# Layer 0's adaLN scale and shift as float32 products on four 32-column strips of TensorE, the first four units pipelined over slices of the scale

## The chip, the cores and the metric

The kernel runs on one core of a Trainium2 chip. The metric is the device time of one execution in microseconds (us). Tensors are float32. Large products are made from two rounded halves of each operand (`hh`, `hl` for the activations, `wh`, `wl` for the weights), as three matmuls `hh*wh + hl*wh + hh*wl` that accumulate in PSUM; "a product" of a unit below is one such matmul.

## The reference, cut to what matters

Two layers, each on 512 latent and 256 context tokens of width 2048:

```python
mod = jax.nn.silu(cond) @ w_ada + b_ada            # cond: c for the latents, c_ctx for the context
shift, scale, gate = jnp.split(mod, 3, axis=-1)    # 3 x 2048 values for each of the two
h = rms_norm(x, norm_w) * (1 + scale) + shift
p = h @ w_in                                       # 2048 x 6144: pool, gates, q, k, v
...                                                # pooling mixer and differential attention
x = x + gate * (merged @ w_out)
```

The change touches `scale` and `shift` of layer 0 alone: two vectors of 2048 values, each the product of a 2 x 2048 matrix (the two conditions) with a 2048 x 2048 block of `w_ada` (16.8 MB).

## The kernel before

The weights `w_in` are cut into 48 units of 128 columns for each layer; a unit is 16 steps over the contraction (k), each with three products for 512 latent and three for 256 context tokens, 96 matmuls in all. `ordered` (L66) chains everything on TensorE into the order in which the program issues it, and adds the cost of each to a planned clock. Side streams (generators) get a turn in `tick` when that clock has passed their due time. The kernel is scheduled at build time into one fixed order for each engine; each engine's queue, and SyncE's queue of DMA issues, runs strictly in that order.

**Start (`startup`, L885).** The order is a string of steps, `SS` (L1160). The scale comes in eight slices of 256 channels (`front(c)`, L929). `SK` makes them by turns in two ways. Slices 0, 2, 4, 6 ("P") load `w_sc0` and multiply on TensorE: per slice 16 float32 matmuls with two weight columns (the two conditions), tile `ads`, a row copy on ScalarE (`adr`) and two transposes (`adt`). Slices 1, 3, 5, 7 ("S") load the transposed `w_sct0` as eight 128 x 512 tiles; VectorE multiplies and sums each for one condition (`asq`, L953), GpSimd multiplies for the other (L957), and ScalarE sums that (L958). `fin(c)` (L980) closes a slice: bias, `acol`, then `hh`, `hl` of two k-steps from `xT` (L994 on ScalarE, L995 on VectorE). `proj` multiplies units 0 to 3 for these k-steps into `su` and `su_sc` (PSUM), since all four are accumulated at once. `N` computes the RMS roots from the squares (`ssq`), `S` spreads them over the tokens (`rsb`, `rstd`). `K` does the last three k-steps and evacuates (`vp`, L724).

**Shift (`shift_stream`, L272, over `mod_sums`, L212).** A side stream that begins at `H`, near the start's end. For each of 64 tiles of 128 x 512 (`swsh`) VectorE multiplies and sums for one condition (`jksh`, L258), GpSimd multiplies for the other (L260) and ScalarE sums (L261). The 64 sums close in groups of four channel blocks into two extra columns of `hh` and `hl` (columns 768 and 769). Units 4 to 7 (pooling values) need no shift. The first gate unit, unit 8 (`pj` with 258 columns), does.

**Pooling.** After each pooling unit, `pool_front` runs window sums on VectorE (two of eight on GpSimd); `pool_mix` multiplies them by `pool_w` (`mx`) and ScalarE evacuates (`M`). Weights of a unit are split by ScalarE (`wh_i`, L167) and VectorE (`wl_i`, L168). From unit 8 on, `gate_rows` and later `scale_shift` use `mod_sums` for the other adaLN parts.

Of the kernel before, what the change touches and what calls it, by code (L numbers as in the profile page):

```python
# [38 lines left out]
def tile_hybrid_block(ctx: ExitStack, tc, xc, xt, cc, w_in, w_out, w_sc0, w_sct0, w_sh0, w_mod0, w_mod1, b_col, norm_col,  # L39
# [99 lines left out]
    nc.vector.tensor_tensor(csil, csil, ctmp, ALU.mult)  # L139

# [71 lines left out]
    def mod_sums(nm, srcs, conds, tot, close, pace=None, extra=None):  # L212
        n = len(srcs)
        ahead = [0]
# [3 lines left out]
        def load(i):  # L218
            if i < 4 * n:
                ring = extra[1]() if extra else [(wpool, "wa", 2)]  # L220
                pool, tag, bufs = ring[i % len(ring)]
                ahead[0] = len(ring) - 1 if extra else 1
                w = pool.tile([P, 512], F32, tag=tag, name=f"sw{nm}_{i}", bufs=bufs)
                (queued if extra else behind)(nc.sync.dma_start(w, srcs[i % n][i // n]))
                tiles[i] = w

        load(0)
        while len(tiles) < ahead[0]:
            load(len(tiles))
        cs = slice(conds[0], conds[-1] + 1)  # L230
        rot = [(wpool, "ac0"), (wpool, "ac1")] + ([(extra[0], "p2")] if extra else [])
        cts = {}

        def load_c(c, s):
            if s < 4:
                pool, tag = rot[(2 * s + c) % 3 if extra else c]
                cts[c, s] = pool.tile([P, 512], F32, tag=tag, name=f"ct{c}_{nm}_{s}")
                (queued if extra else behind)(nc.sync.dma_start(cts[c, s].rearrange("p (k q) -> p k q", q=P),
                                                                csil_d[4 * s:4 * s + 4, c, :].partition_broadcast(P)))

        for s in range(4):
            for c in conds:
                if (c, s) not in cts:
                    load_c(c, s)
            ct = [cts.get((c, s)) for c in range(2)]
            if not (extra and s):
                yield -(SH[1] if extra else LA[3])
            dst = part if s else tot
            for j in range(n):
                i = s * n + j  # L250
                while len(tiles) <= ahead[0] and i + len(tiles) < 4 * n:
                    load(i + len(tiles))
                w = tiles.pop(s * n + j)
                for c in conds:
                    acc = dst[:, j, c:c + 1]
                    scratch = w if c == conds[-1] else (extra[2] if extra else wide_tile)(f"jk{nm}_{s}_{j}")
# [9 lines left out]
                if extra and j in (n // 2, n - 1):  # L266
                    load_c(0 if j < n - 1 else 1, s + 1)
                yield -(pace or LA[phase[0]])
# [5 lines left out]
    def shift_stream(ap, pace, ring, scratch):  # L274
        shcol = const.tile([P, KC, 2], F32, tag="ctmp", name="shcol")

        def close(j):
            v = shcol[:, j:j + 4]
            nc.vector.tensor_tensor(v, v, bcol[:, 0, j:j + 4, 0].unsqueeze(2).to_broadcast([P, 4, 2]), ALU.add)
            for k in range(j, j + 4):  # L280
                split(shcol[:, k, :], hh[k][:, TOK:], hl[k][:, TOK:])
            if j == 12:
                tables[0] = layer_tables(0)

        yield from mod_sums("sh", [w_sh0[j] for j in range(KC)], (0, 1), shcol, close, pace, (ap, ring, scratch))
# [71 lines left out]
    def phase_in(l):  # L357
# [499 lines left out]
    def startup(ap, pj, pscore, units, finish):  # L857
        kinds = SK
# [50 lines left out]
        ring = ["q0", "q1", "k0"]  # L909
        state = {}  # L910
        cnt = {"P": 0, "S": 0}

        def ws_tile(c, k, n):
            r = kinds[c]
            if c == 0 and k < 6:
                if k == 0:
                    state["w0"] = hpool.tile([P, 6, 256], F32, tag="hl0", name="ws0")
                w = state["w0"][:, k:k + n]
                queued(nc.sync.dma_start(w, w_sc0[c, :, k:k + n, :]))
                return w  # L920
            if c == 0 and k >= 12:
                tag = "G1" if k == 12 else "vh"
            else:
                tag = ring[cnt[r] % len(ring)]
                cnt[r] += 1
            w = ap.tile([P, n, 256], F32, tag=tag, name=f"ws{c}_{k}")
            queued(nc.sync.dma_start(w, w_sc0[c, :, k:k + n, :]))
            return w

        def front(c):  # L930
            kind = kinds[c]
            if kind == "P":
                ps = misc(f"ads{c}")
                for k0 in range(0, KC, 3):
                    n = min(3, KC - k0)
                    w = ws_tile(c, k0, n)
                    for j in range(n):
                        k = k0 + j
                        mm(ps[:2, :256], csil[:, k, :], w[:, j, :], k == 0, k == KC - 1)
                    yield  # L940
                row = wpool.tile([P, TOK], F32, tag="wx", name=f"adr{c}")[:2, :256]
                nc.scalar.activation(row, ps[:2, :256], AF.Copy)
                state[c] = row
                return
            acc = const.tile([P, 2, 2, 4], F32, tag="as", name=f"as{c}", bufs=2)
            for s in range(4):
                for j in range(2):
                    pool, tag = ((wpool, "wa"), (ap, "tmp"), (wpool, "ac0"), (wpool, "wa"), (ap, "tmp"), (wpool, "ac1"))[cnt["S"] % 6]
                    cnt["S"] += 1
                    w = pool.tile([P, 512], F32, tag=tag, name=f"ws{c}_{s}{j}", bufs=1 if tag[:2] == "ac" else 2)  # L950
                    queued(nc.sync.dma_start(w, w_sct0[2 * c + j, s]))
                    sq = wpool.tile([P, 512], F32, tag="wp", name=f"asq{c}_{s}{j}")
                    nc.vector.scalar_tensor_tensor(sq, w, 1.0, spread[0, s], ALU.mult, ALU.mult, accum_out=acc[:, j, 0, s:s + 1])  # L953
                    if (2 * s + j) % SD[0] == 1:
                        nc.vector.scalar_tensor_tensor(w, w, 1.0, spread[1, s], ALU.mult, ALU.mult, accum_out=acc[:, j, 1, s:s + 1])
                    else:
                        nc.gpsimd.tensor_tensor(w, w, spread[1, s], ALU.mult)  # L957
                        nc.scalar.activation(w, w, AF.Copy, accum_out=acc[:, j, 1, s:s + 1])  # L958
                    yield
            state[c] = acc  # L960

        spread = {}

        def spread_in():
            for i, (big_, last) in enumerate((("ah", "fq"), ("al", "fk"))):
                t = ap.tile([P, 3, 512], F32, tag=big_, name=f"csB{i}")
                u = ap.tile([P, 512], F32, tag=last, name=f"csC{i}")
                for d, k0, k1 in ((t, 0, 12), (u, 12, 16)):
                    d = d.rearrange("p s (k q) -> p (s k) q", q=P) if k0 == 0 else d.rearrange("p (k q) -> p k q", q=P)
                    queued(nc.sync.dma_start(d, csil_d[k0:k1, i, :].partition_broadcast(P)))  # L970
                for s in range(3):
                    spread[i, s] = t[:, s]
                spread[i, 3] = u

        def fin(c):
            with tc.high_priority(offset=1000):
                a = acol[0][:, 2 * c:2 * c + 2]
                if kinds[c] == "P":
                    pt = misc(f"adt{c}")
                    transposes(pt, [state[c][:, i * P:(i + 1) * P] for i in range(2)], 2)  # L980
                    total = pt[:, :4].rearrange("p (k c) -> p k c", c=2)
                else:
                    total = a
                    nc.vector.tensor_reduce(a, state[c], AX.X, ALU.add)
                nc.vector.tensor_tensor(a, total,
# [295 lines left out]
```

## Time and profile before

| | us |
|---|---|
| three timed runs | 2438.93, 2442.76, 2444.49 |
| their median | 2442.76 |
| the profiled execution, first to last instruction | 2437.6 |
| from start to unit 4's first product | 152.5 |
| from there to unit 8's first product | 117.4 |
| from there to 336 us | 66.1 |
| the rest | 2101.6 |

The page gives no time for the profiled execution other than its span, which is 5.2 us under the median. All times below that name a place are us from the span's start.

How to read it: TensorE (PE) is the engine that sets the end; behind 336 us the program issues the same work in both kernels. So the first three stretches of the table are read one by one: what the engine did there, and what it waited for. A busy share on another engine costs nothing by itself; it costs what PE waits for it.

### The profile page before, as it was taken

The numbers are of one execution on the slowest core, as the hardware profiler recorded it, in microseconds if no ns is written. First come the engines' busy times: TensorE is split into PE (matmuls) and PEld (weight loads), VectorE is DVE, ScalarE is ACT, GpSimd is POOL, SyncE is SP. The second block draws the span as 40 slices with busy tenths as digits, with TensorE's granted clock in tenths as the row PEclk, the third lists the DMA queues.
The fourth block names the chain that finished last, engine by engine and source line by source line (L and its number), as shares of the span: only waits on it lengthen the run. The fifth ranks groups of instructions, "written<-read, shape, count | busy, mean of one in ns | idle before, by whom it ended". The sixth has DMA issues, their size and how long they took to land.

```text
span 2437.6 us, 35303 instructions
## 1 busy us (share of the span) xinstructions
PE 2301.9 (94%) x12411; PEld 1916.9 (79%) x12411; DVE 1568.5 (64%) x2942; ACT 1206.3 (49%) x2586; POOL 637.0 (26%) x574
## 2 busy tenths in 40 slices
PE   6777799999999999998989999999999999999999
PEld 3566688888888888887767788788888888887787
DVE  5799955567767767777533468665666566666433
ACT  4544444455555555656555556223555445555321
POOL 2666645312122122122676720001120000000000
PEclk9888899999999999999999999999999999999999
DMA  8645455433333233234665555564333222224643
GB/s 277 205 154 157 133 172 165 122 104 109 92 102 108 87 111 104 81 90 137 203 192 186 182 174 147 178 193 143 102 115 92 69 66 63 63 68 129 198 135 116
DMA packets 194178, 324.27 MB, mean 133 GB/s; under 512 B 20993, under 2 KB 50257, under 8 KB 194001
## 3 DMA queue, kind: packets, MB, share of 16 engines
q1 hardware_dynamic: 194000, 322.03, 44.1%
q8 instruction: 97, 1.59, 0.3%
q14 instruction: 81, 0.66, 0.1%
HBM read 291.50 MB, written 24.16 MB: 129 GB/s over the span
## 4 chain that ended last, share of the span: by engine, by line
PE 50%; DMA 6%; DVE 4%; ACT 3%; POOL 3%; issue 2%; SPq 0%; DVEq 0%; POOLq 0%; ACTq 0%
PE pj L89 32%; PE ob L89 9%; PE sc L89 3%; DMA swss<-in_w_mod 3%; PE po L89 2%; POOL jkss L260 1%; PE at L98 1%; PE eb L89 1%; POOL swss L260 1%; DMA wr_o<-in_w_out 1%; DMA wr_m<-merged_d 1%; PE qt L98 1%; DMA xr<-in_xc 1%; ACT p L584 1%; DVE wl_i L168 1%
## 5 line engine op out<-in xcount | busy, mean ns | idle before, releaser
L89 PE MATMUL pj<-hh,wh_i 128*128 128x512 f32 (+2 forms) x2368 | 861.3, 364 | 23.4 <-DVE vp L724 16.1
L89 PE MATMUL pj<-hl,wh_i 128*128 128x512 f32 (+2 forms) x2368 | 831.4, 351 | 6.2 <-DVE hl L168 6.2
L89 PE MATMUL pj<-hh,wl_i 128*128 128x512 f32 (+2 forms) x2368 | 832.0, 351 | 1.1 <-DVE wl_i L168 1.1
L89 PEld LDWEIGHTS pj<-hh,wh_i 128*128 128x128 f32 x2368 | 450.7, 190 | 90.6 <-ACT wh_i L167 16.5
L89 PEld LDWEIGHTS pj<-hh,wl_i 128*128 128x128 f32 x2368 | 450.3, 190 | 64.3 <-DVE wl_i L168 1.5
L89 PEld LDWEIGHTS pj<-hl,wh_i 128*128 128x128 f32 x2368 | 451.1, 191 | 58.1 <-DVE hl L168 6.9
L168 DVE TENSOR_TENSOR wl_i<-wr_i,wh_i 128x512 fp32r<-128x512 f32 x352 | 269.9, 772 | 120.2 <-ACT wh_i L167 113.9
L167 ACT ACTIVATE wh_i<-wr_i 128x512 fp32r<-128x512 f32 x352 | 220.0, 628 | 248.9 <-PE pj L89 177.0
L89 PE MATMUL ob<-wh_o,hh 128*128 128x512 f32 x640 | 256.5, 401 | 17.9 <-DVE X L1119 14.3
L89 PE MATMUL ob<-wh_o,hl 128*128 128x512 f32 x640 | 254.5, 398 | 0.0
L89 PE MATMUL ob<-wl_o,hh 128*128 128x512 f32 x640 | 254.3, 397 | 0.0
L260 POOL TENSOR_TENSOR swss<-swss,ct_ss 128x512 f32<-128x512 f32 x128 | 181.5, 1418 | 265.8 <-DVE jkss L258 99.8
L168 DVE TENSOR_TENSOR wl_o<-wr_o,wh_o 128x512 fp32r<-128x512 f32 x144 | 105.1, 732 | 194.0 <-ACT wh_o L167 193.6
L260 POOL TENSOR_TENSOR swg<-swg,ct_g 128x512 f32<-128x512 f32 x88 | 123.3, 1403 | 313.9 <-DMA swg<-in_w_mod 105.6
L584 ACT ACTIVATE p<-sc,st,psc 128x768 f32<-128x768 f32 (+1 forms) x160 | 143.4, 901 | 57.5 <-DVE st L580 32.6
L89 PEld LDWEIGHTS ob<-wh_o,hh 128*128 128x128 f32 x640 | 121.5, 190 | 50.3 <-DVE X L1119 18.0
L579 DVE TENSOR_REDUCE st<-sc 128x2 f32<-128x1536 f32 (+1 forms) x80 | 123.3, 1541 | 58.7 <-PE sc L89 58.4
L167 ACT ACTIVATE wh_o<-wr_o 128x512 fp32r<-128x512 f32 x144 | 90.0, 626 | 131.3 <-PE ob L89 94.0
L89 PEld LDWEIGHTS ob<-wh_o,hl 128*128 128x128 f32 x640 | 121.4, 190 | 28.5
L89 PEld LDWEIGHTS ob<-wl_o,hh 128*128 128x128 f32 x640 | 121.8, 190 | 27.5
L589 POOL COPY r<-st 128x1 f32<-128x1 f32 x80 | 17.1, 214 | 478.8 <-DVE st L586 478.8
L260 POOL TENSOR_TENSOR swsh<-swsh,ct_sh 128x512 f32<-128x512 f32 x64 | 106.5, 1674 | 52.1 <-DVE jksh L258 19.1
(288 smaller groups left out, 3620.1 us busy)
## 6 DMA issues: line engine op xcount, KB each, us to landing
wr_i<-in_w_in SPq DMA_DIRECT2D x352, 256.0 KB, 2.7
wr_o<-in_w_out SPq DMA_DIRECT2D x144, 256.0 KB, 2.8
swg<-in_w_mod SPq DMA_DIRECT2D x128, 256.0 KB, 2.9
swss<-in_w_mod SPq DMA_DIRECT2D x128, 256.0 KB, 2.9
swsh<-in_w_sh SPq DMA_DIRECT2D x64, 256.0 KB, 2.8
ws<-in_w_sct SPq DMA_DIRECT2D x32, 256.0 KB, 5.0
wr_m<-merged_d SPq DMA_DIRECT2D x32, 256.0 KB, 2.7
wr_e<-in_w_in SPq DMA_DIRECT2D x32, 256.0 KB, 2.8
```

Of the source, the lines that this page charges most:

```text
L89: ordered(nc.tensor.matmul(out, a, b, start=start, stop=stop), c)
L98: ordered(nc.tensor.transpose(pt[:, j * w:(j + 1) * w], a, ident[:a.shape[0], :a.shape[0]]), 0.109)
L167: nc.scalar.activation(hi, src, AF.Copy)
L168: nc.vector.tensor_tensor(lo, src, hi.bitcast(F32), ALU.subtract)
L260: behind(nc.gpsimd.tensor_tensor(scratch, w, ct[c], ALU.mult))
L579: nc.vector.tensor_reduce(st[:, 0:2], ps[:, :, :nk], AX.X, ALU.max)
L584: nc.scalar.activation(pp[:, :nk], ps[:, n, :nk], AF.Exp, bias=st[:, n:n + 1], scale=psc[:, qt, n:n + 1], accum_out=st[:, 2 + n:3 + n])
L589: nc.gpsimd.tensor_copy(r1[:, qt:qt + 1], st[:, 4:5])
```

## The change

All eight slices of the scale, and all of the shift, are now float32 products on TensorE with 32 weight columns in place of 2. `csil32` holds the two conditions in columns 0 and 1 and zeros in the other 30. `vec` puts the product of step k on the output partitions `32*(k%4)` to `32*(k%4)+31`, so the 16 steps of a slice accumulate into four separate strips of 32 columns of the array. `fold` (four small identity blocks added) then sums the four strips: one 128 x 128 by 128 x 2 product for each 128 channels takes the place of the transposes.

```diff
+    def vec(out, k, w, start, stop):
+        g = k % 4
+        ordered(nc.tensor.matmul(out[32 * g:32 * g + 32], csil32[:, k, :], w, start=start, stop=stop),
+                2 * (w.free_size() / 2400.0 + 0.0025))
...
+    csil32 = wpool.tile([P, KC, 32], F32, tag="ac0", name="csil32")
+    nc.gpsimd.memset(csil32, 0.0)
+    nc.vector.tensor_scalar(csil32[:, :, :2], csil, 1.0, None, ALU.mult)
+    fold = const.tile([P, 2], F32, name="fold")
...
+    def columns(pt, row, n):
+        for i in range(n):
+            mm(pt[:, 2 * i:2 * i + 2], row[:, i * P:(i + 1) * P], fold, True, True)
...
-    def shift_stream(ap, pace, ring, scratch):
+    def shift_stream(pscore, ap, pace):
...
-        yield from mod_sums("sh", [w_sh0[j] for j in range(KC)], (0, 1), shcol, close, pace, (ap, ring, scratch))
+        ring = [(wpool, "wa", 2), (ap, "tmp", 2), (wpool, "ac1", 1), (wpool, "wa", 2), (ap, "tmp", 2)]
...
+        for _ in range(len(ring)):
+            load()
+        yield -SH[1]
+        acc = pscore.tile([P, 4, 512], F32, tag="sc", name="shacc")
+        for b in range(4):
+            for c in range(2):
+                for k0 in range(0, KC, 4):
+                    for k in range(k0, k0 + 4):
+                        i = (2 * b + c) * 8 + k // 2
+                        vec(acc[:, b, c * 256:(c + 1) * 256], k, tiles[i][:, k % 2, :], c == 0 and k < 4, c == 1 and k >= KC - 4)
+                    load()
+                    load()
+                    yield -pace
+            row = wpool.tile([P, 512], F32, tag="wp", name=f"shr{b}")
+            nc.scalar.activation(row, acc[:, b], AF.Copy)
+            yield pace
+            pt = misc(f"sht{b}")
+            columns(pt, row, 4)
...
         def front(c):
-            kind = kinds[c]
-            if kind == "P":
...
+            ps = misc(f"ads{c}")
+            k0 = 0
+            for n, tag in ((5, "ah"), (3, None), (5, "al"), (3, None)):
...
+                w = ap.tile([P, n, 256], F32, tag=tag, name=f"ws{c}_{k0}")
+                queued(nc.sync.dma_start(w, w_sc0[c, :, k0:k0 + n, :]))
+                for k in range(k0, k0 + n):
+                    vec(ps[:, :256], k, w[:, k - k0, :], k < 4, k >= KC - 4)
...
                 yield from proj(7, (-1, 0, 1), us)
+                if us[0] == 0:
+                    norm_spread()
...
-    SS = "x0 a q0 s0 f0|x1 b c F0 f1|f2 A0|B0 s1 F1 A1 q1 x2 x3 x4 s2 s3|B1 F2 f3|f4 d x5|A2 F3 B2 s4 q2 F4 x6|A3 s5 B3|f6|f5 x7 A4 f7 F5 B4|s6 q3 s7 N F6 A5 B5 F7 H S A6 K"
+    SS = ("f0 c x0 q0 s0 f1 x1 F0 A0 a F1 s1 B0 f2 x2 q1 A1 F2 s2 B1 f3 x3 A2 F3 s3 B2 f4 x4 q2 A3 F4 s4 B3 "
+          "f5 x5 d A4 F5 s5 B4 f6 x6 q3 A5 F6 s6 B5 f7 x7 F7 s7 A6 N K H")
-    SH = [0.97, 4.61, 30.18, 6]
+    SH = [2.2, 6.0, 30.18]
```

In `SS`, f is a slice's products, F its close, A and B the two k-steps of units 0 to 3 that it allows, x and q the loads of activations and weights, s the squares. The loads of a slice go into four buffers, two of which (`ah`, `al`) are the same for every slice, so a slice's first load waits for the first five products of the slice before it. The shift has five buffers of 256 KB, reloaded two at a time after every four products.

TensorE at the start. Before, slices 0 and 1 (`ads`, weight columns by 256) stand in a row, with the transposes `adt` between them:

```order
L204 MATMUL csilT<-ident,csil 32x128
L89 MATMUL ads_153<-ws_154,csil 2x256 x6
L89 MATMUL ads_153<-ws_6_163,csil 2x256 x3
L89 MATMUL ads_153<-ws_9_168,csil 2x256 x3
L89 MATMUL ads_153<-ws_12_173,csil 2x256 x3
L89 MATMUL ads_153<-ws_15_178,csil 2x256
L98 MATMUL adt_193<-ident,adr_181 128x2 x2
L89 MATMUL ads_214<-ws_0_215,csil 2x256 x3
```

Now, the same place (the first `su` rows are unit 0 at k-step 0):

```order
L94 MATMUL ads_121<-ws_0_122,csil_83 32x256 x5
L94 MATMUL ads_121<-ws_5_129,csil_83 32x256 x3
L94 MATMUL ads_121<-ws_8_134,csil_83 32x256 x5
L94 MATMUL ads_121<-ws_13_141,csil_83 32x256 x3
L94 MATMUL ads_181<-ws_0_182,csil_83 32x256 x5
L94 MATMUL ads_181<-ws_5_189,csil_83 32x256 x3
L94 MATMUL ads_181<-ws_8_194,csil_83 32x256 x5
L94 MATMUL ads_181<-ws_13_201,csil_83 32x256 x3
L89 MATMUL adt_211<-fold,adr_146 128x2 x2
L89 MATMUL su_118<-hh_100,wh_s_0_155 128x512
L89 MATMUL su_118<-hl_216,wh_s_0_155 128x512
```

Both slices are done ahead of the first unit product, the close of slice 0 stands behind slice 1's products, and from there each slice stands between the k-steps of two slices earlier and one slice earlier.

TensorE in unit 4. Before, its products follow each other (`hh`, `hl` are the activations of a k-step):

```order
L89 MATMUL pj_4_0_1357<-hh_95,wh_i_4_2_1319 128x512
L89 MATMUL pj_4_0_1357<-hl_866,wh_i_4_2_1319 128x512
L89 MATMUL pj_4_0_1357<-hh_95,wl_i_4_2_1320 128x512
L89 MATMUL pj_4_0_1357<-hh_96,wh_i_4_3_1325 128x512
L89 MATMUL pj_4_0_1357<-hl_955,wh_i_4_3_1325 128x512
```

Now four shift products (`shacc`, two for each loaded tile `wsh`) stand among them:

```order
L89 MATMUL pj_4_0_1185<-hl_705,wh_i_4_2_1147 128x512
L89 MATMUL pj_4_0_1185<-hh_102,wl_i_4_2_1148 128x512
L94 MATMUL shacc<-wsh_1190,csil_83 32x256 x2
L94 MATMUL shacc<-wsh_1192,csil_83 32x256 x2
L89 MATMUL pj_4_0_1185<-hh_102,wh_i_4_2_1147 128x512
```

There are 32 such groups of four: 24 among the products of units 4 to 7, and the last eight in one row (`shacc` 32 times) between unit 7's last product and unit 8's first.

VectorE as the units 0 and 1 are evacuated. Before, the shift's `jksh` stands between the steps of `pool_front` (`s`, `pl`) and ahead of the evacuation of unit 2 (`vp_2`):

```order
L714 SCALAR_TENSOR_TENSOR s_0_0_1_1145<-s_0_0_1_1145,vp_0_1137 128x256
L258 SCALAR_TENSOR_TENSOR jksh_7_1210,shcol<-swsh_1128,ct_sh_1046 128x512
L258 SCALAR_TENSOR_TENSOR jksh_8_1222,shcol<-swsh_1184,ct_sh_1046 128x512
L168 TENSOR_TENSOR pl_0_1144<-s_0_0_1_1145,ph_0_1143 128x512
L168 TENSOR_TENSOR pl_0_1144<-s_0_0_1_1145,ph_0_1143 128x256
L258 SCALAR_TENSOR_TENSOR jksh_9_1236,shcol<-swsh_1196,ct_sh_1046 128x512
L724 TENSOR_TENSOR vp_2_1255<-su_sc,rstd 128x512
```

Now, the same place:

```order
L742 SCALAR_TENSOR_TENSOR s_0_0_1_1011<-s_0_0_1_1011,vp_0_1003 128x256
L187 TENSOR_TENSOR pl_0_1010<-s_0_0_1_1011,ph_0_1009 128x512
L187 TENSOR_TENSOR pl_0_1010<-s_0_0_1_1011,ph_0_1009 128x256
L739 TENSOR_TENSOR s_0_1_1_1029<-s_0_1_1_1029,edge 128x1
L187 TENSOR_TENSOR wl_i_4_3_1154<-wr_i_4_3_1151,wh_i_4_3_1153 128x512
L740 TENSOR_TENSOR s_0_1_1_1029<-s_0_1_1_1029,edge 128x1
```

The shift has left VectorE's queue, and GpSimd's and ScalarE's with it; only a row copy on ScalarE and the splits of 16 pairs of columns remain of it there.

## Rows read from the trace of the kernel before

**Rows 1.** page: the span of the profiled execution, the first line

```profile
span 2437.6 us, 35303 instructions
```

**Rows 2.** windows: length, busy PE, PEld, DVE, ACT, POOL, clock, DMA share, GB/s

```profile
0.00:152.50 152.50, 114.17 (x538) 78.41 (x539) 105.83 (x198) 72.75 (x151) 71.55 (x62) 0.91 0.69 227
152.50:269.90 117.40, 84.44 (x441) 71.98 (x439) 116.27 (x179) 49.82 (x126) 81.42 (x61) 0.87 0.51 150
269.90:336.00 66.10, 56.74 (x294) 49.02 (x295) 52.08 (x104) 33.48 (x92) 37.95 (x30) 0.87 0.46 145
```

**Rows 3.** waits of PE, 0 to 152.5 us: total, times, longest

```profile
PE ads L89 <- DMA ws<-in_w_sc: 19.2, 5, 12.7
PE su_sc L89 <- DVE vp L724: 3.6, 1, 3.6
PE ssq L89 <- DVE xsum L879: 3.0, 1, 3.0
```

**Rows 4.** waits of PE, 152.5 to 269.9 us

```profile
PE pj L89 <- DVE vp L724: 16.1, 2, 10.3
PE mx L89 <- ACT M L747: 15.7, 3, 12.3
```

**Rows 5.** waits of PE, 269.95 to 336 us

```profile
PE pj L89 <- DVE hl L168: 6.2, 3, 4.1
PE pj L89 <- ACT hh L167: 2.9, 2, 2.3
```

**Rows 6.** groups, 152.5 to 269.9 us: count, busy us, mean ns, idle before

```profile
L260 POOL TENSOR_TENSOR swsh<-swsh,ct_sh 128x512 f32<-128x512 f32 x46 | 76.9, 1684 | 34.0 <-DVE jksh L258 13.2 <-DMA ct_sh<-csil_d 9.2 <-ACT swsh L261 8.1
L258 DVE SCALAR_TENSOR_TENSOR jksh<-swsh,ct_sh 128x512 f32<-128x512 f32 x45 | 47.6, 1059 | 0.2
L168 DVE TENSOR_TENSOR wl_i<-wr_i,wh_i 128x512 fp32r<-128x512 f32 x14 | 19.8, 1420 | 0.5 <-ACT wh_i L167 0.5
```

**Rows 7.** page, costliest groups: the same split over the whole span

```profile
L168 DVE TENSOR_TENSOR wl_i<-wr_i,wh_i 128x512 fp32r<-128x512 f32 x352 | 269.9, 772 | 120.2 <-ACT wh_i L167 113.9
```

**Rows 8.** timeline of PE: first matmul of unit 4, first behind it

```profile
152.49 0.39 PE L89 MATMUL pj<-hh,wh_i 128*128 128x512 f32 x1
...
169.37 0.39 PE L89 MATMUL mx<-ph,wh_pw 128*128 128x512 f32 x1
```

**Rows 9.** groups of PE, 0 to 130 us: the scale products of four slices

```profile
L89 PE MATMUL ads<-ws,csil 128*2 128x256 f32 x128 | 34.0, 424 | 19.2 <-DMA ws<-in_w_sc 19.2
```

**Rows 10.** timeline of PE: scale products in a row, and between unit products

```profile
58.46 4.05 PE L89 MATMUL ads<-ws,csil 128*2 128x256 f32 x18
...
88.81 0.28 PE L89 MATMUL su_sc<-hh,wl_s 128*128 128x256 f32 x1
89.02 1.46 PE L89 MATMUL ads<-ws,csil 128*2 128x256 f32 x6
...
90.75 0.40 PE L89 MATMUL su<-hl,wh_s 128*128 128x512 f32 x1
```

**Rows 11.** timeline of PE: four score products, four on 64-row strips, next

```profile
500.48 0.86 PE L89 MATMUL sc<-k,q 128*128 128x512 f32 x4
501.27 0.61 PE L89 MATMUL sc<-kl,q 64*128 64x512 f32 x4
501.81 0.50 PE L89 MATMUL pj<-hh,wh_i 128*128 128x512 f32 x1
```

**Rows 12.** timeline of PEld: one weight load of the scale products

```profile
18.07 0.13 PEld L89 LDWEIGHTS ads<-ws,csil 128*2 128x2 f32 x1 [0.30 <-issue]
```

**Rows 13.** windows: the ten us in which loads run with nothing else

```profile
10.00:20.00 10.00, 3.17 (x8) 0.99 (x9) 3.18 (x6) 2.31 (x3) 0.00 (x0) 1.00 0.98 321
```

**Rows 14.** DMA issues: KB each, median us to landing

```profile
swsh<-in_w_sh SPq DMA_DIRECT2D x64, 256.0 KB, 2.8
```

**Rows 15.** timeline of PE: start after a slice closes, and one-column products

```profile
78.74 0.50 PE L89 MATMUL su<-hh,wh_s 128*128 128x512 f32 x1 [1.96 <-ACT hh L994]
...
111.78 1.47 PE L89 MATMUL ssq<-ones,xsum 128*128 128x1 f32 x12 [2.98 <-DVE xsum L879]
```

More of the change, by code (lines that the diff above doesn't have):

```diff
@@ L210, in wide_tile, with mod_sums @@
         return wpool.tile([P, 512], F32, tag="wp", name=nm)
-    def mod_sums(nm, srcs, conds, tot, close, pace=None, extra=None):
+    def mod_sums(nm, srcs, conds, tot, close):
         n = len(srcs)
-        ahead = [0]
         part = const.tile([P, 2 * KC, 2], F32, tag="part", name=f"part_{nm}")
@@ L219, in load @@
             if i < 4 * n:
[L220 to L224, printed above, removed]
+                w = wpool.tile([P, 512], F32, tag="wa", name=f"sw{nm}_{i}", bufs=2)
+                behind(nc.sync.dma_start(w, srcs[i % n][i // n]))
                 tiles[i] = w
         load(0)
-        while len(tiles) < ahead[0]:
-            load(len(tiles))
         cs = slice(conds[0], conds[-1] + 1)
[L231 to L239, printed above, removed]
         for s in range(4):
+            ct = {}
             for c in conds:
[L243 to L247, printed above, removed]
+                ct[c] = wpool.tile([P, 512], F32, tag=f"ac{c}", name=f"ct{c}_{nm}_{s}")
+                behind(nc.sync.dma_start(ct[c].rearrange("p (k q) -> p k q", q=P),
+                                         csil_d[4 * s:4 * s + 4, c, :].partition_broadcast(P)))
+            yield -LA[3]
             dst = part if s else tot
@@ L250, in mod_sums @@
                 i = s * n + j
-                while len(tiles) <= ahead[0] and i + len(tiles) < 4 * n:
+                while len(tiles) <= 1 and i + len(tiles) < 4 * n:
                     load(i + len(tiles))
-                w = tiles.pop(s * n + j)
+                w = tiles.pop(i)
                 for c in conds:
                     acc = dst[:, j, c:c + 1]
-                    scratch = w if c == conds[-1] else (extra[2] if extra else wide_tile)(f"jk{nm}_{s}_{j}")
+                    scratch = w if c == conds[-1] else wide_tile(f"jk{nm}_{s}_{j}")
                     if MODE[phase[0]][c if len(conds) > 1 else 2] == "D":
@@ L265, in mod_sums @@
                     close(j - 3)
-                if extra and j in (n // 2, n - 1):
-                    load_c(0 if j < n - 1 else 1, s + 1)
-                yield -(pace or LA[phase[0]])
+                yield -LA[phase[0]]
             if 0 < s < 3:
@@ L272, in tile_hybrid_block, with load @@
     tables = {}
-    def shift_stream(ap, pace, ring, scratch):
+    def shift_stream(pscore, ap, pace):
         shcol = const.tile([P, KC, 2], F32, tag="ctmp", name="shcol")
[L277 to L283, printed above, removed]
-        yield from mod_sums("sh", [w_sh0[j] for j in range(KC)], (0, 1), shcol, close, pace, (ap, ring, scratch))
+        ring = [(wpool, "wa", 2), (ap, "tmp", 2), (wpool, "ac1", 1), (wpool, "wa", 2), (ap, "tmp", 2)]
+        tiles = []
+        total = 8 * KC // 2
+        def load():
+            i = len(tiles)
+            if i < total:
+                pool, tag, bufs = ring[i % len(ring)]
+                w = pool.tile([P, 2, 256], F32, tag=tag, name=f"wsh{i}", bufs=bufs)
+                queued(nc.sync.dma_start(w, w_sh0[i // 8, :, 2 * (i % 8):2 * (i % 8) + 2, :]))
+                tiles.append(w)
+        for _ in range(len(ring)):
[16 more added lines that the diff above has]
+            columns(pt, row, 4)
+            k = 4 * b
+            nc.vector.tensor_tensor(shcol[:, k:k + 4], pt[:, :8].rearrange("p (k c) -> p k c", c=2),
+                                    bcol[:, 0, k:k + 4, 0].unsqueeze(2).to_broadcast([P, 4, 2]), ALU.add)
+            for j in range(k, k + 4):
+                split(shcol[:, j, :], hh[j][:, TOK:], hl[j][:, TOK:])
+            yield -0.1
+        tables[0] = layer_tables(0)
     def scale_shift():
@@ L930, in front @@
-        def front(c):
-            kind = kinds[c]
-            if kind == "P":
[L933 to L973, printed above, removed]
+        rows = {}
@@ L977, in fin @@
                 a = acol[0][:, 2 * c:2 * c + 2]
[L978 to L985, printed above, removed]
+                pt = misc(f"adt{c}")
+                columns(pt, rows[c], 2)
+                nc.vector.tensor_tensor(a, pt[:, :4].rearrange("p (k c) -> p k c", c=2),
                                         bcol[:, 0, 2 * c:2 * c + 2, 1].unsqueeze(2).to_broadcast([P, 2, 2]), ALU.add)
```

51 lines of the change are left out of this document (18 added, 33 removed).

## The prediction

> **What bounds the kernel now.** TensorE sets the end, so I read the windows first, to find the stretches in which it isn't full, then its waits there, and last the groups of the engines that it waits for. The span is 2437.6 us [rows 1], 5.2 under the median of the runs; I take that difference as fixed, make the sum in span time and take it off the median. Three stretches matter [rows 2]. In the start (152.5 us) PE is busy 114 us. It waits 19.2 us for scale weights, since the first of them lands 12.7 us after its only earlier work, and 3.0 and 3.6 us for the squares and for the evacuation of units 0 and 1 [rows 3]. In the second stretch (units 4 to 7, 117.4 us) it is busy 84 us and VectorE 116, which is all of it [rows 2]. So VectorE bounds there: PE waits 16.1 us for `vp`, and 15.7 for `M`, which ScalarE evacuates behind the shift's sums [rows 4]. Of VectorE's time 47.6 us are the shift's `jksh`, and beside GpSimd's 76.9 us of `swsh` its other work is slow too: a weight split takes 1.42 us there [rows 6], against 0.77 over the whole span [rows 7]. In the third (66.1 us) unit 8 waits 9.1 us for the shift's columns [rows 5], and the granted clock is 0.87, as in the second [rows 2]. The three together are 336 us; behind them the work is the same.
>
> **The price of a strip product.** The trace of before has no column strips; this is the cost to be bounded. Its float32 products on 2 columns give two records each (128 for 64 products [rows 9]), and 18 records take 4.05 us where 6 take 1.46 [rows 10], so 2.59/12 = 0.216 us a record, 0.43 a product. If strips don't overlap, 0.43 stays. If all four run at once, it is 0.108. The nearest row is the four score products on two 64-row strips: the next matmul starts 0.54 us after their first, while four of the same lengths on the full array take 0.79 (500.48 to 501.27) [rows 11]. So matmuls on different strips do run beside each other. I take that matmuls start in their order: the second record of a step needs the same strip as its first and waits for it, and the first record of the next step can start beside it. That leaves one record's time a step, **0.216 us**, half of before, and both ends stay in the range.
>
> A rule of the Trainium skill speaks against this (TensorE: Matmul & The Clock Gate, Part 3, "The mechanism"): a weight load overlaps running matmuls only if its row group differs, and all strips here use the same 128 rows. Against it, the weight loads of the scale products use the same rows too, and one of 0.13 us [rows 12] is followed and preceded by products without a gap. By the rule the time would be that of the last rival below. The same page's table "Measured speedup vs the span model" gives 2.38 times for three column strips; no run here shows that; by it a step would take some 0.14 us (an estimate), and the sum would be 17 us less.
>
> Entering and leaving the narrow products costs too: from 88.81 to 90.75 lie one 256-column product, six records and one 512-column product [rows 10]. A unit takes 16.88 us [rows 8] for 48 pairs of 512 and 256 columns, so a pair is 0.352 and its parts 0.235 and 0.117; 1.94 - 0.117 - 1.30 - 0.235 leaves **0.29 us a switch**. A `fold` product is a full weight load and two columns; its nearest row is `ssq`, 12 records in 1.47 us [rows 15], so 0.245 for two records.
>
> **The start.** Removed are VectorE's, GpSimd's and ScalarE's sums for four slices, and the transposes; all loads of scale weights now feed PE. The first scale load is issued right behind the conditions. Building `csil32` and `fold` is hidden behind its landing; without that cover it would cost 1 or 2 us. By the new order unit 0 can begin when slices 0 and 1 (2.10 MB each), two pairs of activations (0.79 each) and four weight tiles (1.05) have landed: 6.83 MB at the 321 GB/s that loads reach when nothing else runs [rows 13] is 21.3 us. With 1 us ahead, 2.8 for the last landing [rows 14], 1 or 2 for a weight buffer that SyncE waits for, and some 3 for the squares in front of ScalarE's `hh` (before, 2.0 us of wait for `hh` at such a close [rows 15]), that is 30. Then PE does 4 units (67.5), six slices of 16 steps (20.7), six switches (1.7), seven closes of two folds and a switch (5.5), `ssq` and `rsb` (1.5 and some 1.3), and waits as before for squares and `vp` (6.6; both stand in the same places). 30 + 67.5 + 20.7 + 1.7 + 5.5 + 2.8 + 6.6 = 134.8, so the start gets **17.7 us shorter**. The loads keep pace: a slice, its activations and half a quarter's weights are 3.41 MB or 10.6 us, and PE's period is 8.4 + 3.5 + 0.3 + 0.8 = 13.0. The buffers `ah` and `al` allow this, since they come free with the slice before, a period ahead.
>
> **Units 4 to 7.** The shift's 128 steps come onto PE: 27.6 us, 25 switches (24 groups and one row of eight) 7.3, and four closes of four folds 5.1. Behind each group on PE's queue wait the unit's products, and a reload waits on SyncE for the products that free its buffer, with the units' weight loads behind it. For the 24 groups that lie apart the five buffers give a lead of two groups, over 5 us, and a load lands in 2.8 [rows 14]: hidden. The row of eight isn't: 11 tiles after the five that are there need 9.0 us, the products 6.9, and with a landing at the head PE waits some 4. In return VectorE is rid of 47.6 us and GpSimd of 76.9 [rows 6], so the 31.8 us of waits [rows 4] go but for some 3 of evacuations. Units 67.5, three mixes of a quarter unit 12.7, shift 40.0, waits 7: 127.2 against 117.4, **9.8 us longer**. What is late next there is PE itself.
>
> **Unit 8 and on.** The shift is done before unit 8's first product, and its context half, the first to need it, comes 11 us later, so 9.1 us of waits [rows 5] go. At a granted clock of 0.87 a quarter of the 66.1 us is at half clock, 17 us, of which I put 9 on those waits; the other 8 hold 4 us of loss, that go with the waits that made the clock fall. Half a mix (2 us) has moved ahead. **15.1 us shorter.**
>
> **The sum** is -17.7 + 9.8 - 15.1 = -23.0 us: 2442.8 - 23.0 = **2420 us**. Its own range: unit 0 begins at 26 to 36, waits in the start 3 to 13, in the middle 0 to 14, and the last gain 9 to 17: 2404 to 2436.
>
> **Rivals.** (1) *All strips at once*, 0.108 a step: 224 steps that count (96 in the start, 128 of the shift) lose 24 us, and the row of eight waits 3 longer for its loads: 2399. For it: the strips are independent. Against it: two records a step on one strip.
> (2) *Shift loads not hidden.* Before, GpSimd and ScalarE waited for shift tiles; now PE does, in its fixed order, and SyncE's queue mixes these reloads with the units' weights. If a group waits as long as the four shorter of the five waits for scale weights, 1.6 us each [rows 3], 24 groups cost 39 us: 2459, slower. It decides from 0.95 us a group. Against it: the DMA share was 0.51 there [rows 2], and 16.8 MB more than the units' 6 in 127 us is under 190 GB/s.
> (3) *Strips don't overlap*, 0.43 a step: 224 times 0.216 is 48, less the 4 us wait that it covers: 2464, slower. For it: only row strips are in the trace, and column strips need several moving streams at once. It decides from 0.32 a step.
> (4) *The same with weight loads laid bare*: 448 records with a load of 0.13 [rows 12] at half clock, so 29 to 58 us more: 2493 to 2522. The skill's rule above would give this.
> (5) *The start isn't freed*: SyncE's queue stands at a buffer that ScalarE or VectorE frees late, and slices arrive no sooner than before. The start gives nothing: 2438, no change.
>
> **How the numbers follow.** About 0.2%, 5 us, is what a measurement of this kernel can tell from no change. Forecast 0.62, (1) 0.06, (2) 0.12, (3) 0.10, (4) 0.04, (5) 0.06. Faster: the forecast, (1), a third of (2) and (5): 0.74; slower: (3), (4) and some of (2): 0.19; the same 0.07. The range reaches from (1) into the lower half of (2), 2398 to 2448, and leaves out (3), (4) and the worse part of (2).
>
> **What would show it.** Right: strip products in a row 0.216 us apart with pairs that start together (0.108 a record); unit 4's first product at 135, unit 8's at 262, no `vp`, `M` or `hl` wait over 4 us between, a weight split on VectorE near 0.7. Wrong: 0.4 us or more a step; waits of `shacc` for loads in most groups; unit 0 behind 36 us; a clock that still falls in units 4 to 7.

## The result, and the profile after

| | before | after |
|---|---|---|
| median of four runs, us | 2442.49 | 2397.34 |
| lowest and highest, us | 2438.93 to 2444.49 | 2395.1 to 2401.02 |
| span of the profiled execution, us | 2437.6 | 2393.7 |

The ratio is 0.982, with a 95% interval of 0.981 to 0.984: 45 us faster, where 23 were forecast, and 0.7 us beneath the forecast's range.

The windows of the changed kernel, cut at the same three places of the program as [rows 2] (unit 4's first product, unit 8's first product, and what stood at 336 us). Columns: length, then the busy time of PE, PEld, DVE, ACT and POOL with their instructions, the granted clock (the trace's clock records begin at 32.2 us; the view counts what lies ahead as 1.00), the DMA share and GB/s.

```profile
0.00:125.50 125.50, 102.14 (x690) 78.44 (x691) 53.94 (x111) 50.17 (x85) 16.21 (x28) 0.97 0.68 245
125.50:245.90 120.40, 113.35 (x747) 79.49 (x745) 53.00 (x118) 28.41 (x61) 4.06 (x16) 0.97 0.57 176
245.90:292.30 46.40, 46.40 (x277) 41.16 (x278) 22.00 (x45) 19.09 (x45) 15.86 (x17) 1.00 0.39 122
```

The three stretches are 27.0 us shorter, 3.0 longer and 19.7 shorter: together 43.7 of the 43.9 us that the span lost. Behind them nothing was gained or lost. VectorE, which filled the second stretch before, is busy for 53 of its 120 us, and GpSimd for 4.

What PE waits for in the first stretch (the first four rows) and in the second (the last three); in the third there is no wait at all. Columns: total, times, longest.

```profile
PE ads L94 <- DMA ws<-in_w_sc: 17.3, 5, 9.5
PE su_sc L89 <- DVE vp L752: 2.4, 1, 2.4
PE su L89 <- ACT hh L969: 2.0, 1, 2.0
PE adt L89 <- ACT adr L953: 1.6, 1, 1.6
...
PE shacc L94 <- DMA wsh<-in_w_sh: 4.6, 6, 1.6
PE sht L89 <- ACT shr L303: 1.6, 2, 0.8
PE mx L89 <- ACT M L775: 0.7, 1, 0.7
```

The 31.8 us that PE waited for `vp` and `M` [rows 4] are 0.7 now, and the 9.1 for the shift's columns [rows 5] are gone. All waits for shift tiles belong to the row of eight groups ahead of unit 8.

PE's timeline (start, duration, operation, shape, records): unit 0's first product, a slice between units, unit 4's first product, one shift group among products, and the row of eight.

```profile
27.56 0.79 PE L89 MATMUL su<-hh,wh_s 128*128 128x512 f32 x1 [1.96 <-ACT hh L969]
...
39.14 1.93 PE L94 MATMUL ads<-ws,csil 128*32 128x256 f32 x32
...
125.47 0.39 PE L89 MATMUL pj<-hh,wh_i 128*128 128x512 f32 x1
...
132.89 0.40 PE L89 MATMUL pj<-hh,wl_i 128*128 128x512 f32 x1
133.22 0.64 PE L94 MATMUL shacc<-wsh,csil 128*32 128x256 f32 x8
133.79 0.50 PE L89 MATMUL pj<-hh,wh_i 128*128 128x512 f32 x1
134.12 0.39 PE L89 MATMUL pj<-hl,wh_i 128*128 128x512 f32 x1
...
228.42 0.85 PE L94 MATMUL shacc<-wsh,csil 128*32 128x256 f32 x8
230.09 1.07 PE L94 MATMUL shacc<-wsh,csil 128*32 128x256 f32 x4 [0.82 <-DMA wsh<-in_w_sh]
232.74 3.09 PE L94 MATMUL shacc<-wsh,csil 128*32 128x256 f32 x16 [1.58 <-DMA wsh<-in_w_sh]
...
244.95 1.05 PE L89 MATMUL sht<-fold,shr 128*128 128x2 f32 x8 [0.76 <-ACT shr L303]
```

A step is one product of the contraction, on one strip, and shows as two records. A slice of 16 steps takes 1.93 us to the end of its last product, and a group of four 0.64. In the trace the 32 records of the slice stand in eight fours: the four of one start within 20 ns, and the fours are 0.216 us apart. So a step costs 0.108 us (eight fours for 16 steps). Around a group, from 132.89 to 134.12, lie 1.23 us; without two 512-column products (0.23 each, as their neighbours start) and the group's 0.43 that leaves 0.34 for the switch.

Two groups of 125.5 to 245.9 us (count, busy, mean ns of one, idle before): the weight split on VectorE, and the weight loads of the shift's products.

```profile
L187 DVE TENSOR_TENSOR wl_i<-wr_i,wh_i 128x512 fp32r<-128x512 f32 x18 | 12.5, 692 | 21.0 <-ACT wh_i L186 18.7 <-PE pj L89 2.1
L94 PEld LDWEIGHTS shacc<-wsh,csil 128*32 128x32 f32 x256 | 6.3, 110 | 19.2 <-DMA wsh<-in_w_sh 12.6 <-issue 4.7 <-DMA wr_i<-in_w_in 0.4
```

A split takes 692 ns, against 1420 in [rows 6]. The 256 weight loads of 110 ns would be 28 us one after the other, and fill 6.3: so weight loads of different strips lie beside each other.

### The profile page after: what moved, and what is told of

Same layout as the page of the kernel before. It is cut to its first block, busy times and chain, and to the rows that moved or that the text cites. A ratio compares the mean times of both kernels' runs of the same rounds, so it can differ in the third digit from the quotient of the medians.

```text
span 2393.7 us, 35507 instructions
## 1 busy us (share of the span) xinstructions
PE 2308.7 (96%) x12851; PEld 1916.9 (80%) x12851; DVE 1425.7 (60%) x2736; ACT 1147.7 (48%) x2410; POOL 481.8 (20%) x483
## 4 chain that ended last, share of the span: by engine, by line
PE 54%; DMA 5%; DVE 4%; ACT 3%; issue 2%; POOL 2%; SPq 0%; DVEq 0%; ACTq 0%; POOLq 0%
PE pj L89 32%; PE ob L89 12%; PE sc L89 3%; PE po L89 2%; DMA swss<-in_w_mod 1%; PE eb L89 1%; DMA wr_o<-in_w_out 1%; PE at L104 1%; DMA wr_m<-merged_d 1%; POOL jkss L263 1%; POOL swss L263 1%; PE qt L104 1%; ACT p L612 1%; DVE hl L187 1%; PE mx L89 0%
## 5 line engine op out<-in xcount | busy, mean ns | idle before, releaser
L187 DVE TENSOR_TENSOR wl_i<-wr_i,wh_i 128x512 fp32r<-128x512 f32 x352 | 259.5, 742 | 149.3 <-ACT wh_i L186 141.1
L89 PE MATMUL ob<-wh_o,hh 128*128 128x512 f32 x640 | 255.7, 400 | 22.9 <-DVE X L1089 17.7
L263 POOL TENSOR_TENSOR swss<-swss,ct_ss 128x512 f32<-128x512 f32 x128 | 181.7, 1420 | 266.9 <-DVE jkss L261 98.3
L263 POOL TENSOR_TENSOR swg<-swg,ct_g 128x512 f32<-128x512 f32 x88 | 120.5, 1371 | 323.6 <-DVE jkg L261 91.3
L264 ACT ACTIVATE swss<-swss 128x512 f32<-128x512 f32 x128 | 80.4, 628 | 61.3 <-POOL swss L263 59.0
```

The lines of the kernel that those rows point to most:

```text
L89: ordered(nc.tensor.matmul(out, a, b, start=start, stop=stop), c)
L187: nc.vector.tensor_tensor(lo, src, hi.bitcast(F32), ALU.subtract)
```

## The experiments

The kernel before ran beside all ten on the same chips, at 2439.9 to 2441.6 us. The theory after the result is that all four strips multiply at once, that the shift's departure frees VectorE, and that the clock comes back with it. The rivals are that the strips matter little and the gain is the freed engines', or that the start or the shift alone brought all of it.

One table for all, since a mechanism is read better from a landmark near it than from the end. The first score product (`sc`) is behind everything that was changed. Each landmark is read from one profile of its kernel, and the start alone differs by 4 us between executions (last section).

| kernel | median of runs | unit 4's first product | first score product | from there to the end of the span |
|---|---|---|---|---|
| before | 2442.5 | 152.5 | 500.5 | 1937.1 |
| after | 2397.3 | 125.5 | 457.9 | 1935.8 |
| one strip | 2460.0 | 154.9 | 517.7 | 1938.9 |
| runs of four | 2441.3 | 135.9 | 499.0 | 1936.4 |
| two strips | 2411.9 | 123.9 | 470.1 | 1945.0 |
| slices in runs of two | 2395.5 | 122.3 | 455.8 | 1935.5 |
| scale alone | 2419.4 | 130.1 | 476.4 | 1941.9 |
| shift alone | 2429.2 | 150.5 | 482.6 | 1946.6 |
| pace 1.6 | 2390.4 | 121.5 | 446.7 | 1938.7 |
| start order | 2395.2 | 121.4 | 456.8 | 1935.3 |
| pace 1.6 and start order | 2389.7 | 124.0 | 449.6 | 1939.4 |
| pace 1.3 | 2386.7 | 127.4 | 445.5 | 1942.1 |

### What a strip is worth

**One strip.** Everything stands as after, but all steps use strip 0. (This excerpt and the next two show the choice of the strip alone; the flags that open and close a strip's sum follow it, and with one strip the row copy and the fold take its 32 rows.)

```diff
-        g = k % 4
+        g = 0
```

> All steps go to one strip of 32 columns; the fold sums 32 rows. If the gain of the change comes from the strips running beside each other: 0.43 us a step, 224 times 0.324 is 73 us more, less some 10 hidden: 2455 to 2465, slower than before. If it comes from taking work off VectorE and GpSimd, with TensorE having had the room: under 2442.

**Two strips in turns.**

```diff
-        g = k % 4
+        g = k % 2 + 2 * (k // 8)
```

> Steps go by turns to two strips only (0 and 1 for the first eight, 2 and 3 for the rest). If the price of a step is one record's 0.216 us times two records, divided by the strips in turn: 0.216 us a step, 224 times 0.108 is 24 us more, less up to 10 that hide in the waits for shift loads: 2411 to 2421. If two strips are already as good as four, because a limit other than the strips holds the four: 2397.

**Four strips, in runs of four steps.**

```diff
-        g = k % 4
+        g = k // 4
```

> Steps 0 to 3 of a slice go to strip 0, 4 to 7 to strip 1 and so on, all else as in the changed kernel. Theory A (the matmul engine starts a record only if its strip is free and not far out of its order, so only neighbours on different strips overlap): 0.38 to 0.43 us a step in place of 0.108; 224 steps that count lose some 60 us, of which up to 10 hide in the waits for shift loads: 2445 to 2458. Theory B (records wait for their own strip alone, and any strip's next record may start): 0.108 us a step as now, 2397.

Measured: one strip 2460.02 us (ratio to before 1.008, 1.007 to 1.010), two 2411.94 (0.988, 0.986 to 0.990), runs of four 2441.28 (1.0005, 0.9995 to 1.0014). A slice and a shift group in each, from PE's timelines; first one strip:

```profile
42.09 7.09 PE L94 MATMUL ads<-ws,csil 128*32 128x256 f32 x32
...
162.61 1.91 PE L94 MATMUL shacc<-wsh,csil 128*32 128x256 f32 x8
```

two strips:

```profile
37.67 2.82 PE L94 MATMUL ads<-ws,csil 128*32 128x256 f32 x32
...
142.99 1.06 PE L94 MATMUL shacc<-wsh,csil 128*32 128x256 f32 x8
```

runs of four:

```profile
39.92 4.59 PE L94 MATMUL ads<-ws,csil 128*32 128x256 f32 x32
...
143.64 1.91 PE L94 MATMUL shacc<-wsh,csil 128*32 128x256 f32 x8
```

The last product's end lies 0.16 to 0.2 us behind the pace of the others; without that one strip takes 0.43 us a step. (The slice on two strips is under half of 7.09, because its second eight steps stand on the other two strips and begin while the first two are at work; the group has no such turn.) Six slices and 32 groups cost one strip 6 x 5.16 + 32 x 1.27 = 71.6 us over the changed kernel. Its first score product is 59.8 later: eight of the groups stand in the row ahead of unit 8, and that row is no longer than in the changed kernel (288.19 to 304.11 us, 15.9 against 16.5), so their 10.2 us hide in its waits for loads. So TensorE alone loses 17 us at that landmark against the kernel before, freed engines and all; the strips make the gain. Two strips cost 24 x 0.42 = 10.1 us in the groups that stand apart; the row takes 15.9 us here too. Units 4 to 7 are 9.1 longer (129.5 against 120.4). From unit 4 to the first score product it is 13.8, the other 4.7 lying behind unit 8, where the clock is 0.93 in the first 46.6 us. The 6 x 0.89 in its slices don't show in its start, which is 1.6 shorter (the last section says why).

In runs of four the group stands on one strip and has the price of one strip. Its slice does not: 4.59 us is well under 7.09, so strips do overlap where a run of one ends and the next begins. Neither theory came true: the time is 4 us under the range of theory A, and the groups alone had its price. How far the overlap reaches was open.

**Slices in runs of two**, the shift as after.

```diff
-    def vec(out, k, w, start, stop):
+    def vec(out, k, w, start, stop, run=1):
...
-        g = k % 4
+        g = k // run % 4
...
-                    vec(ps[:, :256], k, w[:, k - k0, :], k < 4, k >= KC - 4)
+                    vec(ps[:, :256], k, w[:, k - k0, :], k < 8 and k % 2 == 0, k >= 8 and k % 2 == 1, 2)
```

> Only the eight slices of the scale change: their steps go to the strips in runs of two (steps 0 and 1 on strip 0, 2 and 3 on strip 1), the shift stays as it is in the changed kernel. In the profiles so far a slice of 16 steps takes 1.93 us when each step is on another strip than the one before, 2.82 with two strips in turns, 4.59 with runs of four steps and 7.09 on one strip. Theory A, the engine starts products ahead over several records, so that a run of two is bridged: a slice takes 1.9 to 2.2 us and the time stays within 2395 to 2400. Theory B, only the last step of a run lies beside the next strip's first: a slice takes 3.3 to 3.7 us; the start has six slices on the path, 1.6 us more each, so 2403 to 2409. Slack of the start's loads could hide some of it.

```profile
37.34 1.97 PE L94 MATMUL ads<-ws,csil 128*32 128x256 f32 x32
48.35 1.97 PE L94 MATMUL ads<-ws,csil 128*32 128x256 f32 x32
```

Theory A: 1.97 us for a slice, 2395.51 us (0.982, 0.979 to 0.984), the same as after. Runs of two are bridged, runs of four are not. So products of a later strip start ahead of products that stand before them on a strip still at work. That each engine's queue runs strictly in the program's order, as said of the kernel before, does not hold of TensorE's starts. The starts in the traces say more: in the slice in runs of two, four records start within 40 ns from the first one on, while in runs of four the first strip's records run alone for 0.887 us, until its third step starts, and from there two strips run. That fits an engine in which one step can wait for each strip, and the next for that strip holds up all behind it; no run tested this by itself.

The Trainium skill says that matmuls start and end strictly in program order (TensorE: Matmul & The Clock Gate, Part 3, "The mechanism"). The ends in a trace are modelled; of the starts, the slice in runs of two shows the contrary. In order, the second product of each run would start 0.43 us behind the first and ahead of the next strip's, so eight runs would take 3.4 us or more.

### The two halves of the change

**Scale alone**: the new slices and start order, with the shift on VectorE, GpSimd and ScalarE as before (of both edits, only the first line and the pace are shown; `H` stands where each shift had it).

```diff
-    def shift_stream(pscore, ap, pace):
+    def shift_stream(ap, pace, ring, scratch):
...
-    SH = [2.2, 6.0, 30.18]
+    SH = [0.97, 4.61, 30.18, 6]
```

> The scale as changed (strips, new order of the start), the shift as before on VectorE, GpSimd and ScalarE. If the start's gain of 27 us stands by itself: unit 4 begins near 125 us, the two stretches behind it as before: 2414 to 2417. If the shift, whose length VectorE sets, then ends no earlier against unit 8 and unit 8 waits longer: 2425 or more.

**Shift alone**: the old start, with the shift's products on the strips.

```diff
-    def shift_stream(ap, pace, ring, scratch):
+    def shift_stream(pscore, ap, pace):
...
-    SH = [0.97, 4.61, 30.18, 6]
+    SH = [2.2, 6.0, 30.18]
```

> The scale as before (half of it on VectorE and GpSimd, old order of the start), the shift as changed on strips. If the two parts add up, the two stretches behind the start get the 17 us shorter that they did in the changed kernel: 2425. If the shift's place on TensorE gives nothing by itself (it costs there what it frees): 2440 or more. If it also frees the start's end, where the old shift had begun: 2418.

Measured: 2419.38 us (0.991, 0.990 to 0.993) and 2429.24 (0.995, 0.993 to 0.997), both 2 us or more slower than the expectation in which the parts add up (2414 to 2417, and 2425). At the first score product they stand 24.1 and 17.9 us ahead of the kernel before, in sum 42.0, and the whole change 42.5: there the halves add up, as far as single profiles can tell. At the end the medians give 20.5 and 12.3, in sum 33, and the whole 45; by the intervals 27 to 42 against 40 to 47, which do touch. What is missing lies behind the first score product, where the program is the same in all of them, and the last column of the table runs from 1935 to 1947 us. Why the two halves stand at its long end stays open.

PE's waits from 120 to 260 us with the scale alone:

```profile
PE pj L89 <- DVE vp L743: 16.9, 2, 10.7
PE mx L89 <- ACT M L766: 13.7, 3, 8.5
```

These are the waits of [rows 4], 16.1 and 15.7 us, hardly changed. With the shift alone they are gone, and the windows, cut at its unit 4, its unit 8 and 316.9 us (as many products behind unit 8's first as 292.3 in the changed kernel), read

```profile
0.00:150.50 150.50, 112.54 (x537) 78.02 (x538) 97.19 (x186) 67.29 (x137) 61.39 (x56) 0.93 0.66 218
150.50:270.50 120.00, 112.42 (x747) 79.27 (x745) 53.18 (x119) 28.57 (x61) 4.03 (x16) 1.00 0.56 177
270.50:316.90 46.40, 46.40 (x278) 41.14 (x278) 21.24 (x45) 18.99 (x45) 17.66 (x18) 1.00 0.40 123
```

So the shift's sums made these waits, and with them goes the clock of 0.87 in both stretches [rows 2]. The second and the third stretch are as long as in the changed kernel (120.0 and 46.4 us); the gain of the shift stands behind unit 8.

### The row of eight, and the start's order

**Pace 1.6**: the groups come closer, so that fewer are left over at unit 8.

```diff
-    SH = [2.2, 6.0, 30.18]
+    SH = [1.6, 6.0, 30.18]
```

> The shift's groups come due after 1.6 planned us in place of 2.2, so that none is left for a row ahead of unit 8. In the changed kernel the last eight groups take 17 us there, where eight groups among unit products cost 5. If that row is bound by its loads because they have nothing to hide behind: 9 to 12 us less, 2386. If the loads can't be had any faster wherever the groups stand: waits of the shift products for loads spread over units 4 to 7, and 2395 to 2400.

**Start order**: slice 1's loads ahead of the first activations.

```diff
-    SS = ("f0 c x0 q0 s0 f1 x1 F0 A0 a F1 ...
+    SS = ("f0 c x0 f1 q0 s0 x1 F0 A0 a F1 ...
```

> The loads of slice 1 stand ahead of the first weight tiles of units 0 to 3, the fourth of which SyncE holds until the first is split; slice 0's and 1's loads then run without a gap. If that gap is what unit 0 waits for: it begins at 23 to 25 us in place of 27.6, and the time is 3 to 4 us less, 2394. If the bytes in front of unit 0 are what counts, whatever their order: within 1 us of the changed kernel.

**Both.**

> Both: pace 1.6 and slice 1's loads first. If each is right by itself: 2383. If the start's part gives nothing: as the pace alone, 2386.

**Pace 1.3.**

```diff
-    SH = [2.2, 6.0, 30.18]
+    SH = [1.3, 6.0, 30.18]
```

> The pace of the shift's groups is 1.3 in place of 2.2 (1.6 in the earlier run, which left two groups in a row at the end, 5.0 us for some 1.3 us of products and folds). Now the last group stands among unit 7's products, and only the folds stand ahead of unit 8. If the loads keep pace at the closer spacing: no wait of a shift product for a load over 0.5 us, 2386 to 2389. If the closer groups come at the loads' limit, waits of a product for a load appear in the middle groups, some 0.5 us each: 2390 to 2398.

Measured: pace 1.6 2390.4 us (0.979, 0.977 to 0.981), start order 2395.2 (0.981, 0.980 to 0.983), both 2389.73 (0.978, 0.976 to 0.980), pace 1.3 2386.68 (0.978, 0.976 to 0.980). Pace 1.6 gained 7 us where 9 to 12 were expected. At pace 1.6 the row is down to two groups:

```profile
227.89 1.06 PE L94 MATMUL shacc<-wsh,csil 128*32 128x256 f32 x12
230.02 0.62 PE L94 MATMUL shacc<-wsh,csil 128*32 128x256 f32 x4 [1.07 <-DMA wsh<-in_w_sh]
231.68 1.05 PE L89 MATMUL sht<-fold,shr 128*128 128x2 f32 x8 [1.03 <-ACT shr L303]
232.60 0.48 PE L89 MATMUL pj<-hh,wh_i 128*128 128x512 f32 x1
```

From unit 4's first product to unit 8's are 111.1 us (121.51 to 232.60) against 120.4 after: the row of eight cost 9 us, and closer groups cost nothing elsewhere, so in units 4 to 7 the loads are hidden. Pace 1.3 takes the last row away too: there no shift product waits for a load, and units 4 to 7 take 110.3 us. Its gain over 1.6 is within what can be measured; its gain over the changed kernel, 10.7 us, is not. Its median is the lowest of all versions.

What makes the row slow is its loads: with one strip or two it is as long as with four (15.9 us against 16.5). The DMA issues of the changed kernel, 222 to 246 us (count, KB each, median us to landing):

```profile
wsh<-in_w_sh SPq DMA_DIRECT2D x16, 256.0 KB, 4.2
```

Each reload waits for the products that free its buffer, and lands 4.2 us later, where I had taken 2.8 [rows 14]. At best five tiles come in such a turn, and 11 are wanted behind the first five; unit 8's first weights lie between them in SyncE's queue. But until the last tile lands, 13.9 us into the row, the DMA engines are also busy for 0.89 of the time (third line of the windows; 0.98 where loads run alone [rows 13]). Whether the way round the buffers or the engines' rate bounds the row was not tested apart. At the end of the first wait the granted clock fell to 0.50, or 1.2 GHz, and it stayed there until 236.9 us (second line):

```profile
228.40:245.00 16.60, 11.04 (x66) 2.62 (x66) 6.81 (x18) 2.65 (x8) 0.00 (x0) 0.79 0.80 260
232.50:236.00 3.50, 3.09 (x16) 0.75 (x16) 2.80 (x9) 0.94 (x2) 0.00 (x0) 0.50 0.92 324
228.40:242.30 13.90, 9.12 (x54) 2.14 (x55) 6.81 (x18) 2.05 (x7) 0.00 (x0) 0.75 0.89 289
```

With the new start order unit 0 begins at 23.6 us, 4.0 earlier, and unit 4 at 121.4, 4.1 earlier; but only 1.1 of it is left at the first score product, and 2 of it in the medians, within the intervals of the two. Beside pace 1.6 it brings nothing. That the gap ahead of unit 0 matters was not shown.

## Why the prediction was right in sign and short in size

**The bound, right.** VectorE bounded units 4 to 7 through the shift's sums: scale alone keeps the waits, shift alone removes them, and the split fell to 692 ns (near 0.7 was forecast).

**The price of a strip product, wrong by half.** 0.216 us was forecast, and 0.108 is what a step takes: rival 1, which had a chance of 0.06 and gave 2399. The step that failed is "matmuls start in their order": I let the second record of a step hold back the next step's first. Both ends of the price's range were right: one strip has 0.43, and its 2460 us is 4 from rival 3's 2464. The rule of the Trainium skill on row groups which I weighed (TensorE: Matmul & The Clock Gate, Part 3, "The mechanism") stood for rival 4 (the prediction calls it the last), with 2493 to 2522; the trace contradicts it for column strips: all of them use the same rows, a group holds eight weight loads of 0.11 us, 0.88 in sum, and it takes 0.43 us in all.

**The start, -27.0 where -17.7 was forecast.** Unit 0 began at 27.6 (forecast 30), and the six slices took 96 x 0.108 = 10.4 us (20.7). The waits behind that, 2.4 + 1.6 + 1.0, are 5.0 (6.6). These three make 14.3 us less than the forecast 134.8, so 120.5; 125.5 was measured. Of the 5 us between, 3.4 are the clock at 0.79 and 0.81 in two stretches of 8 and 9 us (0.21 x 8 + 0.19 x 9), a term that I had left out. Another 2.3 are the first twelve products of unit 0, which take 4.5 us (27.56 to 32.03); twelve of the same sizes take 2.2 later, at 1.08 for six from 35.83 on. That is half pace too, ahead of the first clock record.

**Units 4 to 7, +3.0 where +9.8 was forecast.** The products took 13.8 us and not 27.6; a switch 0.34 and not 0.29. The row of eight's wait was mis-sized the other way: 16.5 us for 3.5 us of products, so 13, where I had 4 (7 for rival 1). I had counted 9.0 us for the row's loads, and the last of them landed 13.9 us into it. The other waits, 3 in the forecast, came to 0.7. 127.2 - 13.8 + 9 + 1.2 - 2.3 is 121.3; 120.4 was measured.

**Unit 8 and on, -19.7 where -15.1 was forecast.** The terms were the right ones: 9.1 us of waits [rows 5], the clock and a part of a mix moved ahead. The last two were mis-sized. In the kernel before the clock was at half in two stretches:

```profile
269.90:273.90 4.00, 4.00 (x13) 3.42 (x14) 4.00 (x7) 1.45 (x4) 2.42 (x3) 0.50 0.51 134
294.00:308.40 14.40, 9.35 (x41) 8.56 (x42) 11.54 (x30) 7.73 (x21) 5.65 (x10) 0.53 0.42 131
```

I had put 9 us of this clock on the waits; only 5 of it are idle (14.40 less 9.35). In the other 13 PE multiplies, with 258 columns every 0.215 us where 0.12 is usual, and loses some 6 us, where I had 4. The mix moved ahead is 6 products of 512 columns and 12 of 256, 2.8 us by the prices of the prediction, where I had 2. So 9.1 + 6 + 2.8 = 17.9 of the 19.7; what the other 1.8 are stays open.

**The other rivals.** (2) fell: no group apart waits for its loads, also not at pace 1.6; only the row does. (4) fell with the strip price. (5) fell: slices arrive in time, with 1.0 us of wait for one of six. The range was too narrow at its lower end, since it stopped at rival 1's time with the clock's gain at its forecast size. That rival 1's 2399 lies so near 2397 is in part luck: by its terms units 4 to 7 take 116.4 us and the third stretch gets 15.1 shorter, where 120.4 and 19.7 were measured, and the two errors cancel.

## What to carry to other kernels

Narrow products on a matmul engine pay only if products near each other in the program stand on different strips: here the same arithmetic gave 45 us on four strips, 28 on two, 0 in runs of four and -20 on one, by the choice of strips alone. When work is taken off a shared engine, sum the waits that end and the clock that returns, the clock only for the time in which the engine multiplies. Streamed loads that are left for the end in a row have nothing to hide behind; spreading the groups evenly ahead of it was worth 11 us more.

## What was not expected of the hardware

**Strips run ahead.** Four column strips gave 4.0 times one strip (0.43 to 0.108), also in runs of two; a slice in runs of four gave 1.5 times (7.09 to 4.59). That one waiting step a strip is the depth of this look-ahead fits these runs, and was not tested by itself.

**The start's length differs from execution to execution.** The changed kernel and pace 1.6 have the same program there, and need 125.5 and 121.5 us. The clock differs between them; first the windows of the changed kernel:

```profile
99.00:107.00 8.00, 7.33 (x39) 6.53 (x39) 5.72 (x9) 5.38 (x9) 1.87 (x2) 0.79 0.64 221
117.00:126.00 9.00, 8.51 (x39) 7.31 (x40) 4.61 (x16) 1.57 (x3) 1.86 (x7) 0.81 0.04 16
```

and those of pace 1.6:

```profile
98.00:106.00 8.00, 7.18 (x47) 6.54 (x48) 6.38 (x13) 5.79 (x10) 1.95 (x2) 1.00 0.68 239
114.50:122.00 7.50, 6.91 (x39) 6.06 (x40) 4.67 (x16) 1.57 (x3) 1.86 (x7) 1.00 0.07 25
```

Ahead of the first stretch PE waits 1.6 us for `adr` in the one and 0.8 in the other; ahead of the second 2.4 us for `vp` in both, and still the clock falls in one alone. With two strips that wait for `adr` is 0.5, the clock in both places 1.00, and the start 1.6 us shorter than the changed kernel's though its slices are 5.3 longer. So gains and losses of 4 us in the start can't be read from one profile.

**Products at the lower pace where the view gives 1.00.** The timeline of the changed kernel in unit 0:

```profile
29.47 0.41 PE L89 MATMUL su_sc<-hh,wh_s 128*128 128x256 f32 x1
29.69 0.41 PE L89 MATMUL su_sc<-hl,wh_s 128*128 128x256 f32 x1
...
32.78 0.28 PE L89 MATMUL su_sc<-hh,wh_s 128*128 128x256 f32 x1
32.90 0.28 PE L89 MATMUL su_sc<-hl,wh_s 128*128 128x256 f32 x1
```

The same products start 0.22 us apart first and 0.12 later, and the granted clock is 1.00 in every window from 27 to 35 us. That is no reading: in the trace the clock's records begin at 32.2 us, and the view counts the time ahead of them as full clock. The spacing of the products is what shows the lower pace there, up to 32.0 us.
